# Seven products instead of eight for the second MLP matrix, with its sums on VectorE and by DMA, and a 16-byte pitch of the normed inputs

## The chip, the cores and the metric

One core of a Trainium2 chip runs the whole kernel. The metric is the device time of one execution in microseconds (us). The engines in the text: PE (TensorE, matrix products), DVE (VectorE), ACT (ScalarE), POOL (GpSimd, here only a queue that issues DMAs and a few fills) and SP (SyncE, the queue that issues most DMAs).

## What is computed

One decoder layer for 512 prompt tokens and 8 sample tokens, 520 columns in all, with 1024 features and 4096 inner features of the MLP. The part that the change touches:

```python
x = x + g1 * (merged @ w_out)
h2 = rmsnorm(x, norm2_g) * (1 + sc2) + sh2
ff = square(relu(h2 @ w_ff1)) @ w_ff2        # [1024, 4096], [4096, 1024]
x = x + g2 * ff
y = rmsnorm(x, final_norm_g)
```

Before it stand the input projection `w_in` (64 tiles of 128 output features), two recurrent branches, and their output matrices. Everything is float32.

## The kernel before

Activations lie as features x tokens: a tile is 128 features by 520 columns, `HALF` is 260. A float32 product is made of two-part operands: `whi`, `wlo` of the weights (`_split_w`: a cast on ACT, L68, and a subtraction on DVE, L69) and hi, lo of the activations (`split`, L146 and L147). `products` (L100) then issues three matmuls, hi hi, hi lo and lo hi, for each half of 260 columns, each with its own weight load. `gemm` runs over the inner tiles into one PSUM tile `mm` of two banks (one per half); `pmm` holds two such tiles.

A weight tile is 1024 rows x 128 columns (512 KB). `weights` gets the list of all tiles in the order of their use; `take_w` keeps loads three tiles ahead of the splits and splits two ahead (`AHEAD`). The loads go out on SP's queue into `wst` (four buffers); the split tiles lie in `whl` (two buffers).

The normed input `h` and the second norm's scaled input `h2` are [128, 8, T2] tiles, T2 = 530 floats: 520 columns, then nine columns of shifts and one to fill up. `h2` is scaled by the root mean square only after the product (L891).

`mlp` runs in two halves of the inner features. In a half, 16 tiles of `w_ff1` make 16 inner tiles: product, scale by `rs` (L891), the samples' shift (L892), relu with the prompt's shift (L893, L894), square on DVE (L895), split (L146, L147) into the pool `ab`. Then each of the eight output tiles takes two weight tiles of `w_ff2`, 96 matmuls, and `residual` (L808 and on) adds the gated sum to `x[m]`. In the second half the final norm follows each output tile (`final_tile`: transposes, squares, the product with `gbc`); the last output tile is done half by half of the tokens (`last_tile`), and the rows are scaled and written out.

The order on each engine follows the program's order by priority and readiness, fixed ahead of the run; `urgent` puts what frees a PSUM bank ahead of what was issued shortly before.

## Time and profile before

| | |
|---|---|
| runs | 1074.60, 1074.03, 1071.95 us; median 1074.03 |
| profiled execution | span 1070.9 us from the first to the last instruction |
| PE, PEld | 1035.1 us (97%), 998.7 us (93%) busy |
| DVE, ACT, POOL | 603.9 us (56%), 446.8 us (42%), 25.6 us (2%) busy |
| granted clock of PE | mean 0.996 |
| chain that ended last | PE 93%, of it the matmuls of L100 82% of the span |
| DMA | 136.34 MB, mean 127 GB/s |

A PE row's duration is the latency of one matmul; since matmuls are pipelined, what one costs is the distance between the starts of two. In rows of groups the number after `x` is the count, then busy time in us and the mean of one in ns, then idle time ahead of them and what ended it. In rows in order of time stand start, duration, engine, line, operation and operands (out<-in).

### The profile page before, as it was taken

How to read it: one execution, taken by the hardware profiler on the slowest of the kernel's cores; microseconds unless marked ns; L12 is line 12 of the kernel's file. 1: busy time of each engine (PE TensorE's matmuls, PEld its weight loads, DVE VectorE, ACT ScalarE, POOL GpSimd, SP SyncE). 2: the span in 40 equal slices, each digit the busy share in tenths (PEclk: the TensorE clock that was granted, in tenths of full speed). 3: DMA queues.
4: the chain of work that ended last, by engine and by line, in shares of the span. 5: the costliest groups of instructions: out<-in, count | busy, mean ns of one | idle time of the engine just before them, and what ended most of it. 6: DMA issues, size and time to landing. Idle time of an engine off the chain costs nothing.

```text
span 1070.9 us, 23934 instructions
## 1 busy us (share of the span) xinstructions
PE 1035.1 (97%) x10132; PEld 998.7 (93%) x10132; DVE 603.9 (56%) x1429; ACT 446.8 (42%) x897; POOL 25.6 (2%) x68
## 2 busy tenths in 40 slices
PE   3899999999999999989999999999999999999996
PEld 1799999999999999989999999999999999999996
DVE  6568678596786867464333346665542235554333
ACT  5445744663574364351222234444421124443332
POOL 2200000000000000110000000000000000000000
PEclk9999999999999999999999999999999999999999
DMA  9953444334333324695555573333323333332312
GB/s 278 252 170 101 121 123 125 111 121 141 107 120 113 110 92 142 186 281 165 160 158 160 158 210 86 92 90 89 94 84 99 85 94 93 86 96 82 96 44 80
DMA packets 239212, 136.34 MB, mean 127 GB/s; under 512 B 5214, under 2 KB 233750, under 8 KB 239098
## 3 DMA queue, kind: packets, MB, share of 16 engines
q1 hardware_dynamic: 237218, 129.75, 42.3%
q0 software_dynamic: 1888, 5.07, 1.5%
q8 instruction: 79, 1.29, 0.5%
q14 instruction: 27, 0.22, 0.1%
HBM read 123.61 MB, written 11.26 MB: 126 GB/s over the span
## 4 chain that ended last, share of the span: by engine, by line
PE 93%; SPq 3%; DMA 2%; ACT 1%; DVE 1%; issue 0%; ACTq 0%; DVEq 0%
PE mm L100 82%; PE ps L339 2%; SPq L1061 2%; PE pb L685 1%; DMA wst<-in_w_in_dram 1%; PE ps L544 1%; DMA wm<-in_w_mod_dram 1%; PE pt L628 1%; PE pt L617 1%; SPq L62 1%; PE ps L512 1%; PE pt L630 1%; PE ps L582 0%; PE pt L611 0%; DMA vd<-vs 0%
## 5 line engine op out<-in xcount | busy, mean ns | idle before, releaser
L100 PE MATMUL mm<-h,whi 128*128 128x260 f32 (+1 forms) x3072 | 518.2, 287 | 1.4 <-ACT X L120 1.4
L100 PEld LDWEIGHTS mm<-h,whi 128*128 128x128 f32 x3072 | 432.2, 190 | 7.2 <-issue 3.4
L100 PE MATMUL mm<-h,wlo 128*128 128x260 f32 (+1 forms) x1536 | 318.7, 287 | 0.0
L68 ACT CAST whi<-wst 128x1024 fp32r<-128x1024 f32 x152 | 159.3, 1048 | 333.8 <-PE mm L100 288.4
L69 DVE TENSOR_TENSOR wlo<-wst,whi 128x1024 fp32r<-128x1024 f32 x152 | 185.6, 1221 | 118.7 <-ACT whi L68 116.7
L100 PEld LDWEIGHTS mm<-h,wlo 128*128 128x128 f32 x1536 | 241.4, 190 | 1.7 <-issue 1.0
L100 PE MATMUL mm<-a,whi 128*128 128x260 f32 x1024 | 171.3, 286 | 0.0
L100 PEld LDWEIGHTS mm<-a,whi 128*128 128x128 f32 x1024 | 142.3, 189 | 1.6 <-issue 1.4
L100 PE MATMUL mm<-b,whi 128*128 128x260 f32 x768 | 125.0, 284 | 0.0
L100 PEld LDWEIGHTS mm<-b,whi 128*128 128x128 f32 x768 | 105.9, 189 | 1.6 <-issue 1.6
L100 PE MATMUL mm<-a,wlo 128*128 128x260 f32 x512 | 105.0, 283 | 0.0
L100 PEld LDWEIGHTS mm<-a,wlo 128*128 128x128 f32 x512 | 79.5, 188 | 0.2 <-issue 0.2
L100 PE MATMUL mm<-b,wlo 128*128 128x260 f32 x384 | 78.9, 284 | 0.0
L100 PEld LDWEIGHTS mm<-b,wlo 128*128 128x128 f32 x384 | 59.7, 188 | 0.0
L808 DVE SCALAR_TENSOR_TENSOR ma<-mm,modT,ma 128x260 f32<-128x260 f32 x23 | 11.2, 488 | 70.4 <-PE mm L100 66.0
L893 ACT ACTIVATE t<-t,fsh 128x512 f32<-128x512 f32 x32 | 23.0, 723 | 57.4 <-DVE t L891 57.4
L895 DVE TENSOR_TENSOR t<-t 128x520 f32<-128x520 f32 x32 | 22.3, 700 | 20.9 <-ACT t L894 20.9
L147 DVE TENSOR_TENSOR a<-t,a 128x520 fp32r<-128x520 f32 x32 | 21.9, 696 | 12.8 <-ACT a L146 12.8
L146 ACT CAST a<-t 128x520 fp32r<-128x520 f32 x32 | 19.6, 626 | 18.4 <-DVE t L895 10.0
L796 DVE TENSOR_TENSOR t<-mm,t 128x520 f32<-128x520 f32 x8 | 5.6, 699 | 37.0 <-PE ps L355 37.0
L147 DVE TENSOR_TENSOR b<-t,b 128x520 fp32r<-128x520 f32 x24 | 16.6, 699 | 14.1 <-ACT b L146 14.1
L359 DVE TENSOR_REDUCE mods<-ps 128x9 f32<-128x36 f32 x32 | 6.1, 190 | 32.6 <-PE ps L355 32.5
(301 smaller groups left out, 1008.5 us busy)
## 6 DMA issues: line engine op xcount, KB each, us to landing
wst<-in_w_in_dram SPq DMA_DIRECT2D x64, 512.0 KB
wst<-in_w_ff_dram SPq DMA_DIRECT2D x64, 512.0 KB
wst<-in_w_mod_dram SPq DMA_DIRECT2D x32, 512.0 KB
wm<-in_w_mod_dram SPq DMA_DIRECT2D x16, 512.0 KB
st<-in_state_hgrn_dram SPq DMA_DIRECT2D x8, 512.0 KB
vb<-vd SPq DMA_DIRECT2D x8, 512.0 KB
out_dram<-st SPq DMA_DIRECT2D x8, 512.0 KB
wst<-in_w_branch_a_dram SPq DMA_DIRECT2D x8, 512.0 KB
```

What stands on the lines that cost most here:

```text
L62: self.nc.sync.dma_start(st, src[r0:r0 + 1024, c0:c0 + 128].rearrange("(k p) n -> p k n", p=128))
L68: self.nc.scalar.copy(hi, st)
L69: self.nc.vector.tensor_tensor(lo, st, hi.bitcast(F32), OP.subtract)
L100: self.last_product = self.nc.tensor.matmul(ps[:, s, :c.stop - c.start], x, y[:, c], start=first and n == 0, stop=last and n == 2)
L146: self.nc.scalar.copy(hi, full)
L147: self.nc.vector.tensor_tensor(lo, full, hi.bitcast(F32), OP.subtract)
L339: nc.tensor.matmul(ps[r:r + 32, :n], self.cT[:, k, :], w[:, k, :], start=k < 4, stop=k >= KO - 4)
L512: nc.tensor.matmul(po[j:j + 32, c:c + 128], fkq[:, 2], st[:, b], start=True, stop=True)
L808: nc.vector.scalar_tensor_tensor(x[:, :HALF], ps[:, 0, :HALF], g[:, 0:1], x[:, :HALF], OP.mult, OP.add)
L893: nc.scalar.activation(t[:, :L], t[:, :L], AF.Relu, bias=sh[:, 0:1])
L895: nc.vector.tensor_tensor(t, t, t, OP.mult)
L1061: nc.sync.dma_start(raw[k][:, :, j * 128:(j + 1) * 128], w[r:r + 1024, c:c + 128].rearrange("(k p) n -> p k n", p=128))
```

## The change

Four things change; line numbers in names above are those of the kernel before.

*The second MLP matrix.* Inner features go in four quarters of eight inner tiles. A quarter's inner tiles are taken in four pairs (even, odd tile), the 520 columns as two halves, and the output tiles in four pairs `m`. For each pair of output tiles, seven sums of products take the place of eight. With B11, B12 for the even inner tile's two halves and B21, B22 for the odd one's, `hidden` makes seven forms of a pair of inner tiles, B11, B21, B22, B11 - B12, B12 - B22 - B11, B12 - B22 and B21 + B12 - B22 - B11, each in two parts; the square moves from DVE to ACT (into `f8`). `_split_pair` makes the weights' sums: group 0 is the plain first block, group 1 the plain second column block, group 2 two sums made by accumulating DMAs on POOL's queue (the second overwrites what the first reads, and so waits for it), group 3 two sums on DVE. `product` issues 12 matmuls (4 inner tiles x 3 parts) of 260 columns for product `j`. Products 1, 6, 5, 3 gather in one bank of `mm`, products 7 and 4 in the other, product 2 in the bank `pb`; between them `added` copies the partial sums out (`snap`, ACT, urgent) and adds them to `x`: on DVE, and for two of them a pair in the first three quarters by an accumulating DMA. The samples' columns gather in `zs`.

*The order.* `plan` writes out the order of tiles of the first matrix (`unit`, a quarter of a tile's product) and of products. After a quarter's last tile come the inner tiles 0 to 2 of products 1 of pair 0, 1 of pair 1, 2 and 7 of pair 0, then inner tile 3 of the same four. The next quarter's first tile is cut up between the last products.

*Pools.* Split weight tiles lie in turn in `whl` and in a new pool `sw` (two buffers each). `sw` also holds the raw pairs of `w_ff2` (pair 2's lie in `wst`), loaded as four transfers of 256 KB a pair. Small tiles of the recurrent part move from `sm` and `consts` to `hg` and `hc`, whose place is free again for the MLP.

*Pitch and end.* T2 is 532 floats. The final norm works on pairs of output tiles (`final_pair`), the last pair half by half of the tokens; `gbc` is loaded on SP's queue at the last quarter.

```diff
-NM = 9           # conditioning rows: the prompt and the samples
-T2 = T + NM + 1  # columns with the shifts beside the activations
+NM = 9
+T2 = T + NM + 3
...
+    def split_pool(self):
+        self.nsplit += 1
+        return self.sw if self.sw and self.nsplit % 2 else self.whl
...
+    FORM = {1: 0, 2: 1, 3: 2, 5: 3, 6: 4, 7: 5, 4: 6}
+    GROUP = {1: (0, 0), 2: (1, 0), 4: (1, 1), 7: (2, 0), 5: (2, 1), 6: (3, 1), 3: (3, 0)}
...
+    def plan(self):
+        late, end = (0, 1, 2), (3,)
+        first = [(0, 1), (1, 1), (0, 2), (0, 7)]
+        rest = [(0, 4), (0, 6), (1, 2), (1, 7), (0, 5), (1, 4), (0, 3), (1, 6), (2, 1), (1, 5), (2, 2), (1, 3), (2, 7),
+                (3, 1), (2, 4), (2, 6), (3, 2), (3, 7), (2, 5), (3, 4), (2, 3), (3, 6), 0, (3, 5), 1, (3, 3), 2, 3]
+        items, entries = [], []
+        for q in range(4):
+            items += [("u", q, j, c) for j in range(int(q > 0), KO) for c in range(4)]
+            items += [("p", q, *x, ks) for ks in (late, end) for x in first]
...
+    def _load_pair(self, key):
...
+            for n in range(2):
+                self.nc.sync.dma_start(t[:, 4 * n:4 * n + 4], v[e, :, n])
...
+    def _split_pair(self, key):
+        nc, g = self.nc, key[4]
+        a, b = self.raw[key[1:3]]
+        x11, x21, x12, x22 = a[:, :4], a[:, 4:], b[:, :4], b[:, 4:]
+        if g == 0:
+            hi, lo = (self.sw.tile([128, 4, 128], F32R, name=n, bufs=2) for n in ("xhi", "xlo"))
+            nc.scalar.copy(hi, x11)
+            nc.vector.tensor_tensor(lo, x11, hi.bitcast(F32), OP.subtract)
+            nc.gpsimd.dma_start(x11, x21, accum_op=OP.add)
+            nc.gpsimd.dma_start(x21, x22, accum_op=OP.add)
+            return hi, lo
+        if g == 3:
+            nc.vector.tensor_tensor(x22, x22, x11, OP.add)
+            nc.vector.tensor_tensor(x12, x12, x22, OP.add)
+            del self.raw[key[1:3]]
+        return self._split_w(a if g == 2 else b, self.split_pool())
...
+    def product(self, q, m, j, ks):
...
+        ps = (st["A"] if j == 2 else st["mm"][:, int(j in (7, 4))])[:, :HALF]
+        for k in ks:
+            w, (ah, al) = 4 * part + k if g else k, self.ff[k]
+            f = self.FORM[j]
+            for n, (x, y) in enumerate(((hi, ah), (hi, al), (lo, ah))):
+                self.nc.tensor.matmul(ps, x[:, w], y[:, f], start=j in (1, 7, 2) and k == 0 and n == 0,
+                                      stop=k == 3 and n == 2, skip_group_check=True)
...
+    def hidden(self, q, j, ps):
...
+        f = self.f8
+        nc.scalar.activation(f[:, 2 * e:2 * e + 2], self.two(t), AF.Square)
+        if e == 0:
+            self.forms(*self.ff[k], f[:, 0:1], 0, 1)
+            return
+        self.forms(*self.ff[k], f[:, 2:4], 1, 3)
+        for n, a, op, b in ((6, f[:, 1], OP.subtract, f[:, 3]), (5, f[:, 6], OP.subtract, f[:, 0]),
+                            (7, f[:, 2], OP.add, f[:, 5]), (4, f[:, 0], OP.subtract, f[:, 1])):
+            nc.vector.tensor_tensor(f[:, n], a, b, op)
+        self.forms(*self.ff[k], f[:, 4:8], 3, 7)
+
+    def added(self, q, m, j, ps, s):
...
+        def plus(t, c, part):
+            if q == 3:
+                nc.vector.tensor_tensor(x[t][:, c], x[t][:, c], part, OP.add)
+            else:
+                nc.gpsimd.dma_start(x[t][:, c], part, accum_op=OP.add)
+
+        if j == 1:
+            s[1] = self.snap(ps, "s1", g[0], 2)
+        if j == 7:
+            s[7] = self.snap(ps[:, :n], "s7", g[1], 2)
+            nc.vector.tensor_tensor(zs[1], zs[1], ps[:, n:], OP.add)
...
```

Of the kernel before, what the change touches and what calls it, by code (L numbers as in the profile page):

```python
# [6 lines left out]
F32 = mybir.dt.float32  # L7
# [38 lines left out]
class Kernel:  # L46
# [6 lines left out]
    # ---- weights: a tile is 1024 rows x 128 columns, in two parts that fp32r carries exactly  # L53
    def weights(self, specs):
        self.wspecs = specs
        self.wstage, self.wsplit = {}, {}
        self.wnext_load = self.wnext_split = self.wcur = 0

    def _load_w(self, key, pool):
        src, r0, c0 = key[:3]  # L60
        st = pool.tile([128, KO, 128], F32, name="wst")
        self.nc.sync.dma_start(st, src[r0:r0 + 1024, c0:c0 + 128].rearrange("(k p) n -> p k n", p=128))  # L62
        return st
# [11 lines left out]
    def take_w(self, key):  # L75
        n = self.wcur
        assert self.wspecs[n] == key, (n, self.wspecs[n], key)
        last = n
        for _ in range(AHEAD):  # tiles that go to the products as they are take no place in the split tiles' pool
            last += 1  # L80
            while last < len(self.wspecs) and self.wspecs[last][3:] == (WHOLE,):
                last += 1
        while self.wnext_split < min(last + 1, len(self.wspecs)):
# [4 lines left out]
            whole = self.wspecs[self.wnext_split][3:] == (WHOLE,)  # L88
            self.wsplit[self.wnext_split] = st if whole else self._split_w(st, self.whl)
# [4 lines left out]
    def products(self, ps, w, a, first, last, extra=0, halves=(0, 1)):  # L94
        """ps += W^T a, for one 128 x 128 tile of W and one tile of a, both in two parts."""
# [7 lines left out]
    def gemm(self, keys, acts, extra=0):  # L103
        """[128, 2, HALF (+ extra in the second)] of W^T act for one tile of 128 output features."""
# [10 lines left out]
    # ---- ScalarE's tables: what needs the exponential's and the root's stays together between sigmoids  # L115
# [15 lines left out]
    def urgent(self):  # L131
        """Ahead of what is emitted shortly before: what a product's place in PSUM waits for."""
# [17 lines left out]
    def rsqrt_small(self, x, n, p=128, w=16):  # L150
        """x[p, n] ** -0.5 to float32's accuracy (x normal and positive)."""
# [12 lines left out]
    # ---- constants and parameters  # L164
# [13 lines left out]
    def constants(self):  # L178
        nc, sb = self.nc, self.consts
        # masks of the pairs (s, t) inside 32 x 32 diagonal blocks, by the level that carries them  # L180
# [20 lines left out]
    def transpose_in(self, out, rows, n):  # L201
        """rows [n, 128] -> out [128, n]"""
# [8 lines left out]
    def bounds(self):  # L211
        """What depends on parameters through the exponential: HGRN2's lower bounds, RG-LRU's decay rates."""
# [4 lines left out]
        pl = self.consts.tile([128, 16], F32, name="pl")  # L217
# [3 lines left out]
        sb = self.consts  # L221
# [16 lines left out]
    def decays(self):  # L238
        """c8 = 8 softplus(-lam); log1p(e) = 2 atanh(e / (2 + e))"""
# [15 lines left out]
    def parameters_mod(self):  # L255
        """The norms' scales and the conditioning's bias (plus one where a scale comes of it)."""
# [29 lines left out]
    def parameters_in(self, ra, rb, rc):  # L286
        sb = self.consts
# [13 lines left out]
    # ---- conditioning  # L301
# [9 lines left out]
    def cond(self):  # L311
        """silu of the conditioning rows, transposed, with room for 32 of them."""
# [5 lines left out]
        self.cT = self.consts.tile([128, KO, 32], F32, name="cT")  # L318
# [50 lines left out]
    # ---- the input, its norm, and its transpose  # L369
# [8 lines left out]
    def norm_x(self):  # L378
# [3 lines left out]
        junk = lambda: self.pmm.tile([128, 2, 512], F32, name="mm").rearrange("p a b -> p (a b)")  # noqa: E731  # L382
# [20 lines left out]
    def transposed(self, k):  # L403
        """Columns k * 128 .. + 128 of the rows, transposed where they are."""
# [15 lines left out]
    def affine_split(self, k, prompt, sample):  # L420
        """The normed input's tile k times 1 + scale, plus the shift, in two parts."""
# [7 lines left out]
        v = lambda t: t[:, :L].rearrange("p (t f) -> p t f", f=128)  # noqa: E731  # L429
# [4 lines left out]
    # ---- HGRN2  # L434
# [9 lines left out]
    def head_f(self, h, ps):  # L444
        """f = max(lb, floor) + (1 - lb) sigmoid(fa), k = (1 - lb) sigmoid(-fa)"""
# [43 lines left out]
    def head_sample_v(self, h, v):  # L489
# [3 lines left out]
        vs = self.sm.tile([NB, 128], F32, name="vs")  # L493
# [8 lines left out]
    def head_sample(self, h, st, vb, fkq):  # L502
# [5 lines left out]
        # four samples' states at a time, each with all samples' queries in its own 32 columns of the array  # L508
# [4 lines left out]
        ev = self.sm.tile([128, 256], F32, name="sev")  # L513
# [7 lines left out]
    def head_prompt(self, h, f, X, q, v, og):  # L521
        nc = self.nc
        # values as [s, v]
# [6 lines left out]
        # levels: Q_b[t] = q_t * f's from the b-block's start to t, K_b[s] = k_s * f's after s to the block's end,  # L530
# [634 lines left out]
```

More of the change, by code (lines that the diff above doesn't have):

```diff
@@ L867, in norm2 @@
         nc = self.nc
[L868 to L869 removed]
+        self.rs = self.misc.tile([128, T], F32, name="rs", bufs=1)
+        parts = self.misc.tile([128, 4, T], F32R, tag="f8", name="sqs", bufs=1)
+        parts = parts[:, 0], parts[:, 1]
+        nc.scalar.copy(parts[0], self.sq)
+        nc.vector.tensor_tensor(parts[1], self.sq, parts[0].bitcast(F32), OP.subtract)
         for s in range(2):
@@ new lines, in mlp @@
+    def mlp(self):
+        nc, tc = self.nc, self.tc
+        self.close_pool()
+        self.early.close()
+        self.ffp = self.ctx.enter_context(tc.tile_pool(name="ffp", bufs=1, reuse_waits="tile"))
+        self.zs = self.consts.tile([128, KO, NB], F32, name="zs")
+        nc.vector.memset(self.zs, 0.0)
+        self.ng = self.consts.tile([128, KO], F32, name="ng")
+        nc.vector.tensor_scalar(self.ng, self.modT[:, 40:48, 0], -1.0, None, OP.mult)
+        self.ff, self.pairs, self.taken = {}, {}, {}
+        for what, q, a, b, *ks in self.items:
+            if what == "u":
+                self.unit(q, a, b)
+                continue
+            if (q, a, b, ks[0][0]) == (3, 0, 1, 0):
+                self.final_open()
+            self.product(q, a, b, *ks)
```

323 lines of the change are left out of this document (203 added, 120 removed).

## The prediction

> **What bounds the kernel now.** I read the page first (who is busy, what the chain that ended last consists of), then the busy time by stage, then single rows.
>
> ```profile
> span 1070.9 us, 23934 instructions
> PE 1035.1 (97%) x10132; PEld 998.7 (93%) x10132; DVE 603.9 (56%) x1429; ACT 446.8 (42%) x897; POOL 25.6 (2%) x68
> PE 93%; SPq 3%; DMA 2%; ACT 1%; DVE 1%; issue 0%; ACTq 0%; DVEq 0%
> 690.00:795.00 105.00, 105.00 (x855) 105.00 (x854) 60.40 (x88) 46.18 (x88) 0.00 (x0) 1.00 0.32 91
> 795.00:875.00 80.00, 80.00 (x668) 80.00 (x667) 23.68 (x42) 14.31 (x14) 0.00 (x0) 1.00 0.33 93
> 875.00:970.00 95.00, 95.00 (x771) 95.00 (x771) 54.06 (x80) 41.01 (x80) 0.00 (x0) 1.00 0.32 90
> 970.00:1055.00 85.00, 85.00 (x713) 84.87 (x713) 30.20 (x57) 27.51 (x84) 0.00 (x0) 1.00 0.22 63
> ```
>
> TensorE carries 93% of the chain. The four windows are the MLP: first matrix, second matrix, and both again for the other half of the inner features. Columns are the stretch, then PE, weight load, VectorE, ScalarE and GpSimd busy time, granted clock, DMA share and GB/s. PE is never idle there, the clock is 1.00, VectorE is 30 to 58% busy, GpSimd 0. So each matmul less is worth its issue interval, and each new PE wait costs in full.
>
> **The matmuls removed.** Counts by form, and two beats of the second matrix:
>
> ```profile
> L100 PE MATMUL mm<-a,whi 128*128 128x260 f32 x512 | 86.4, 286 | 0.0
> L100 PE MATMUL mm<-b,whi 128*128 128x260 f32 x512 | 83.0, 282 | 0.0
> L100 PE MATMUL mm<-b,wlo 128*128 128x260 f32 x256 | 53.0, 284 | 0.0
> L100 PE MATMUL mm<-a,wlo 128*128 128x260 f32 x256 | 52.8, 283 | 0.0
> 858.19 0.49 DVE L808 SCALAR_TENSOR_TENSOR ma<-mm,modT,ma 128x260 f32<-128x260 f32 x1 [3.69 <-PE mm L100]
> 869.71 0.49 DVE L808 SCALAR_TENSOR_TENSOR ma<-mm,modT,ma 128x260 f32<-128x260 f32 x1 [3.69 <-PE mm L100]
> ```
>
> These are the 1536 matmuls of the second matrix (512 + 512 + 256 + 256); 286 ns is a latency, not a price. The residual comes every 11.52 us for 96 matmuls, so one costs 120.0 ns. Afterwards there are 4 quarters x 4 pairs x 7 products x 4 inner tiles x 3 parts = 1344, of the same shape (260 columns, own weight load). 192 x 0.120 = **-23.0 us**.
>
> **The pitch.** A normed-input tile starts every 2120 bytes, so every second one is 8 bytes off a multiple of 16; afterwards (2128) none is. Two whole products (a gate on the normed input, then a branch on aligned tiles), and the gate's inner tiles 2 to 5, whose beats start at these times:
>
> ```profile
> 524.66 6.04 PE mm L100 x48
> 531.38 5.96 PE mm L100 x48
> ...
> 526.15 0.65 PE L100 MATMUL mm<-h,whi 128*128 128x260 f32 x4
> 526.87 0.65 PE L100 MATMUL mm<-h,whi 128*128 128x260 f32 x4
> 527.61 0.64 PE L100 MATMUL mm<-h,whi 128*128 128x260 f32 x4
> 528.32 0.66 PE L100 MATMUL mm<-h,whi 128*128 128x260 f32 x4
> 529.07 0.64 PE L100 MATMUL mm<-h,whi 128*128 128x260 f32 x4
> ```
>
> Six matmuls take 0.72 us on tile 2, 0.74 on 3, 0.71 on 4, 0.75 on 5: odd tiles pay up to 5 ns a matmul by these rounded starts; the whole products differ by 0.08 us over 24 odd matmuls, 3.3 ns. 96 products read the normed inputs (64 of w_in, 32 of the first MLP matrix), 2304 odd matmuls. At 2 ns this is **-4.5 us**; ends 0 (the offset isn't the cause) and -7.6 (3.3 ns). I take the low side because a head's chain has other work beside the products.
>
> **What it adds on PE's path.** Durations for these steps:
>
> ```profile
> 876.47 1.23 DVE L69 TENSOR_TENSOR wlo<-wst,whi 128x1024 fp32r<-128x1024 f32 x1 [4.61 <-ACT whi L68]
> 877.62 0.69 DVE L891 TENSOR_TENSOR t<-mm,rs 128x520 f32<-128x520 f32 x1
> 879.20 0.70 DVE L895 TENSOR_TENSOR t<-t 128x520 f32<-128x520 f32 x1 [0.69 <-ACT t L894]
> 880.59 0.70 DVE L147 TENSOR_TENSOR a<-t,a 128x520 fp32r<-128x520 f32 x1 [0.69 <-ACT a L146]
> ...
> 878.34 0.72 ACT L893 ACTIVATE t<-t,fsh 128x512 f32<-128x512 f32 x1 [1.83 <-DVE t L891]
> 879.93 0.63 ACT L146 CAST a<-t 128x520 fp32r<-128x520 f32 x1 [0.77 <-DVE t L895]
> 881.33 1.05 ACT L68 CAST whi<-wst 128x1024 fp32r<-128x1024 f32 x1 [0.78 <-PE mm L100]
> ...
> L875 ACT ACTIVATE rs<-ps,epsc 128x260 f32<-128x260 f32 x2 | 0.8, 472 | 0.0
> L811 DVE TENSOR_TENSOR rst<-mm,modT 128x8 f32<-128x8 f32 x15 | 2.3, 154 | 0.0
> 1061.61 0.41 PE L918 MATMUL ps<-ident,ma 128*128 128x128 f32 x2 [0.67 <-DVE ma L945]
> ```
>
> (1) End of a quarter's first-matrix tiles. Before, 15 other inner tiles came ahead of the last one (90 matmuls, 10.8 us), over a chain of 3.7 us (877.62 to 881.29). Now the last tile must also pass the seven forms, and 36 matmuls on the three older inner tiles plus 9 cover it: 45 x 0.12 = 5.4 us until product 7's last step needs the form B12 - B22 - B11. The chain: scale 0.72, relu with its sample columns 0.75, square 0.63, then four sums on VectorE of half a 520 row each, some 0.36 us apart (1.4), cast of four forms 1.07, their low part 1.2: 5.8 us, plus 0.3 from the last matmul's start to VectorE's. If VectorE does the low part of the first two forms ahead of the sums, as written, 1.2 us more. The stall is 0.6 (sums first) to 2.1 us (as written); an unlucky weight split of 1.2 ahead of it makes 3. I take 1.3, nearer the middle since the order on the engine is by priority: 4 x 1.3 = **+5.2** (2.4 to 12).
>
> (2) Product 4 of pair 0 follows product 7 of pair 0 and adds to the same PSUM bank, which ScalarE must first copy (0.47) and VectorE read (0.15); with the matmul's latency and PE's restart after VectorE (0.15 in the last row: VectorE ended at 1061.46) 1.0 us a quarter: **+4.0** (3 to 6). Other pairs have another pair's product (1.44 us) between.
>
> (3) Splits have four buffers in turn, two ahead. The next quarter's first tile takes the buffer of pair 2's last sums, read until one product before: cast 1.05 + low part 1.2, while PE has 1.44 plus the 0.5 until it needs the low part: 0.7 x 3 = **+2.1** (1 to 5). Three other splits a quarter have 2.9 us for the same 2.3; a VectorE instruction in the way breaks that: 12 x 0.1 = **+1.2** (0 to 7).
>
> (4) The last pair of the last quarter runs products 6, 5, 3 on one bank with nothing between: 0.7 + 0.9 = **+1.6**.
>
> (5) VectorE. A pair costs it four low parts (0.7 + 3 x 1.2), two weight sums of 0.7 and 2.3 us of residual: 8.0, four pairs 32 us of the 45 that PE has in quarters 1 to 3: covered. In the last quarter two residual sums of 0.4 (no DMA), the sample rows (0.6) and the final norm's products (2 x 0.7 + 0.3) come on top: 44 us busy, some 40 in sequence (rows of one engine overlap by 0.08: 876.47 + 1.23 against 877.62), against PE's 39.5 plus the waits above. The cover is nearly gone; I put **+2** (0 to 8). ScalarE stays under 30 us.
>
> (6) The tail behind the last matmul:
>
> ```profile
> 1060.98 0.48 DVE L945 SCALAR_TENSOR_TENSOR ma<-mm,modT,ma 128x252 f32<-128x252 f32 x1
> 1062.05 0.28 ACT L923 ACTIVATE junk<-ps 128x128 f32<-128x128 f32 x1
> 1064.39 0.18 DVE L955 RECIPROCAL fr<-fr 128x3 f32<-128x3 f32 x1 [0.36 <-ACT fr L954]
> 1064.60 1.04 ACT L959 ACTIVATE fx<-fx,fr 128x896 f32<-128x896 f32 x1 [0.25 <-DVE fr L955]
> ```
>
> Two tiles are squared instead of one (2 more at 0.4, and a sample row 0.4), the last row's scale is 1024 wide instead of 896 (+0.15), a separate 128-wide product goes (-0.3): **+0.7** (0 to 2).
>
> (7) The DMA sums: 32 on weights, 24 on residuals, all on GpSimd's queue, where the second sum of a pair waits for the first and holds up what is queued behind (residual sums, the next pair's). Nearest rows, from a stage at twice the traffic:
>
> ```profile
> t<-obT_d POOLq DMA_DIRECT2D x8, 260.0 KB, 7.0
> gbc<-in_final_norm_g_dram POOLq DMA_DIRECT2D x1, 512.0 KB, 5.0
> ```
>
> The tightest are pair 2's: its first split can run when pair 0's first weights are free, 17 us before the split that needs both sums is due (18 us ahead of its product). Two at 5 to 7 us take 10 to 14: **0**. The Trainium skill ("DMA: Bandwidth & Descriptors", section "Anatomy of one DMA") fits 2.0 us plus bytes over 436 GB/s, 2.6 us for 256 KB; the sum would stay the same by it. No run here shows an accumulating transfer yet.
>
> Loads of the second matrix come as 64 transfers of 256 KB instead of 32 of 512 on SP's queue, with DMA 33% busy: 0. The tiles that move to other pools keep their two buffers: 0. In the first-matrix stretches VectorE has 7.2 us of new and old work per 11.8 us: 0.
>
> **Sum**: -23.0 - 4.5 + 5.2 + 4.0 + 2.1 + 1.2 + 1.6 + 2 + 0.7 = -10.7. The runs' median (1074.0) lies 3.1 us above the profiled span of 1070.9; the span becomes 1060.2 and the median 1063.3, say **1064**.
>
> **Rivals.**
> A. The waits are mostly covered (sums ahead of low parts, no VectorE collision): (1) 2.4, (2) 3, (3) 1, (4) 1.4, (5) and (6) 0: 7.8 of 27.5 given back, 1054. For it: VectorE is idle 42% even in the first-matrix stretches. Against: its queue is in order and a split holds it 1.2 us.
> B. VectorE becomes the bound of the product stretches: (1) at 3 each, (3) at 5 + 7, (5) at 8: 12 + 4 + 12 + 1.6 + 8 + 0.7 = 38 lost, +11, 1085 at the far end; half the excess gives no change, 1074. For it: 40 of 39.5 us in the last quarter. Against: the other three have 27% to spare.
> C. Slower, by GpSimd's queue alone: a DMA sum that takes over 8.5 us makes pair 2's second sum late (2 x 8.5 = 17); at 11 us each product 7 of pair 2 waits 5 us and pair 3's, queued behind, as long again: 10 x 4 = 40 us, 1103; it eats the gain of 10.7 from about 10 us a sum on (2.7 us a quarter). For it: 7.0 us rows on that queue. Against: those moved DRAM data at 160 to 210 GB/s; here it is 90. The Trainium skill ("TensorE: Matmul & The Clock Gate", Part 1) has the clock fall to half after an idle window of some 3.4 us; C's waits would then cost more than counted, those of (1) to (4) not. No wait of this length is in this trace's MLP.
> D. The pitch does nothing: 1068.
>
> **Chances.** Forecast 0.48 (1058 to 1069), A 0.22, D 0.08, B 0.14 (half of it within 0.3%), C 0.08. A change of 0.3% (3.2 us) is about what a measurement of this kernel can tell from none. Faster 0.74 (forecast, A, D less their upper ends), same 0.14, slower 0.12. 80% range 1053 (A) to 1076 (half of B); the forecast's own is 1058 to 1069.
>
> **What would show it.** Right: 1344 matmuls on 260-column forms at 120 ns; beats of odd input tiles equal to even ones; PE idle of about a microsecond before product 7's last step and product 4 of pair 0, and at the next quarter's first tile; POOL-queue sums landing within 7 us; VectorE over 85% busy in the last quarter. Wrong: PE waits of 3 us and more behind VectorE's low parts (B) or behind weights that a DMA sum completes (C), or no gaps at all (A).

## The result, and the profile after

| | before | after |
|---|---|---|
| median of the runs, us | 1074.32 (1071.95 to 1074.8) | 1104.16 (1099.81 to 1105.42) |
| ratio, 95% interval | | 1.0281 (1.0256 to 1.0306) |
| span of the profiled execution, us | 1070.9 | 1098.0 |
| mean granted TensorE clock there | 0.996 | 0.981 |

The change makes the kernel 2.8% slower: 30 us by the medians, 27.2 by the profiled executions. The forecast was 10 us faster. From the page of the changed kernel, the busy shares and the rows of PE and of the granted clock in 40 slices:

```profile
PE 1028.7 (94%) x9940; PEld 983.2 (90%) x9940; DVE 694.9 (63%) x1624; ACT 531.4 (48%) x1041; POOL 73.6 (7%) x123
PE   3999999999999999999999999989997899789895
PEclk9999999999999999999999999999998999999898
```

192 instructions fewer on PE, and yet 27 us more span: PE, 97% busy before, is at 94%, and the dents in its row stand in the last third, where the granted clock has its dents too. Busy time by stretch (columns as in the prediction: PE, weight load, VectorE, ScalarE, GpSimd, granted clock, DMA share, GB/s). The first row is the first matrix of quarter 1; the others are the second matrix of quarters 1, 2 and 4:

```profile
676.50:726.50 50.00, 50.00 (x411) 50.00 (x410) 35.95 (x60) 30.71 (x56) 0.00 (x0) 1.00 0.26 75
726.50:777.00 50.50, 41.99 (x307) 40.20 (x306) 30.39 (x55) 22.66 (x35) 12.41 (x15) 0.93 0.60 128
828.00:879.00 51.00, 42.36 (x306) 40.56 (x305) 29.80 (x55) 22.30 (x34) 12.90 (x15) 0.90 0.59 127
1033.00:1085.40 52.40, 45.50 (x344) 43.03 (x343) 35.19 (x84) 30.59 (x99) 3.43 (x4) 0.93 0.12 21
```

The first matrix runs as before: PE full, clock 1.00. In the second PE stands still for 8.5 us of 50 (6.9 of 52 in the last quarter), at a mean clock of 0.90 to 0.93, and no other engine is full: VectorE is busy 60%, in the last quarter 67%. The waits of TensorE's instructions by what released them (us in total, times, longest):

```profile
PE mm L995 <- DVE zs L1071: 12.5, 9, 2.2
PE pb L995 <- ACT ff3h L1007: 8.6, 4, 2.2
PE mm L995 <- DVE ma L1063: 4.1, 7, 0.6
PE mm L995 <- DVE zs L1059: 3.3, 5, 0.8
PE pb L995 <- DVE ma L1063: 2.3, 4, 0.6
PE pb L995 <- DVE ff3l L1008: 1.8, 4, 0.5
PE mm L110 <- DVE wlo L73: 1.0, 3, 0.4
```

The first row is, but for two waits of the last pair, the wait of product 6 for the sum of product 4 (`added`, L1063): the releaser is inferred, and L1071, another pair's product 5, is only the next instruction behind that sum on VectorE. The shorter waits of the same kind stand in the third row, under L1063 itself.

For a ledger I added up the distances between successive matmul starts in the MLP. What a distance has above 0.124 us is a wait if it is more than 0.145 us, and a slow step if it is 0.06 to 0.145 us; the rest is plain distance. A slow step is at half clock if the trace's granted clock is 0.5 there (a matmul then takes 0.22 us); the others are single steps at full clock. From before to after:

| part | us |
|---|---|
| all up to the first matrix (its first 270-column matmul at 682.00, then 676.41) | -5.6 |
| plain distances of the second matrix (1536 matmuls, then 1344) | -20.9 |
| plain distances of the first matrix | -1.8 |
| waits of TensorE (none, then 42) | +42.2 |
| slow steps at half clock (0, then 9.5) | +9.5 |
| slow steps at full clock (1.8, then 3.4) | +1.7 |
| transposes, small distances | -0.4 |
| behind the last matmul (10.2, then 12.6) | +2.4 |
| sum | 27.1 |

So the removed matmuls did save time, and so did the part ahead of the MLP; two things outweighed them. The first row is not the pitch alone. Between the matmuls 4750 and 5000, where TensorE waits for a tile of `w_in`, the changed kernel takes 26.4 us against 30.0 before, and between 6500 and 6750, ahead of the MLP, 28.8 against 27.1. All eleven traces of the changed scheme show it (26.2 to 29.1, and 27.8 to 29.1); with the pitch alone (e1_pitch, e1_again, below) the first is 30.5 and 31.2, the second 27.1. The wait in the chain of before, after and e1_pitch:

```profile
446.68 11.56 DMA wst<-in_w_in_dram
443.81 9.06 DMA wst<-in_w_in_dram
444.32 12.16 DMA wst<-in_w_in_dram
```

Now the waits in the MLP. TensorE's rows around the first quarter's end (start, duration, operands, idle time before and its releaser):

```profile
728.74 0.28 PE L995 MATMUL mm<-ff3h,xlo 128*128 128x260 f32 x1
731.16 0.38 PE L995 MATMUL pb<-ff3h,whi 128*128 128x260 f32 x1 [2.15 <-ACT ff3h L1007]
732.04 0.39 PE L995 MATMUL pb<-ff3l,whi 128*128 128x260 f32 x1 [0.50 <-DVE ff3l L1008]
733.12 0.58 PE L995 MATMUL pb<-ff0h,whi 128*128 128x260 f32 x1 [0.58 <-DVE ma L1063]
733.50 0.42 PE L995 MATMUL pb<-ff0l,whi 128*128 128x260 f32 x1
733.72 0.42 PE L995 MATMUL pb<-ff0h,wlo 128*128 128x260 f32 x1
...
737.45 0.39 PE L995 MATMUL mm<-ff0h,whi 128*128 128x260 f32 x1 [0.76 <-DVE zs L1059]
739.74 0.39 PE L995 MATMUL mm<-ff0h,whi 128*128 128x260 f32 x1 [0.58 <-DVE ma L1063]
```

Product 2 of pair 0 waits 2.31 + 0.76 us for the forms of the last inner tile. What stands ahead of them on VectorE and ScalarE:

```profile
725.09 1.22 DVE L73 TENSOR_TENSOR wlo<-wst,whi 128x1024 fp32r<-128x1024 f32 x1 [0.99 <-ACT whi L72]
726.23 0.69 DVE L1022 TENSOR_TENSOR ft<-mm,rs 128x520 f32<-128x520 f32 x1
...
728.94 0.62 ACT L953 CAST xhi<-wst 128x512 fp32r<-128x512 f32 x1 [0.27 <-PE mm L995]
729.46 0.47 ACT L1003 ACTIVATE s<-mm,modT 128x260 f32<-128x260 f32 x1
729.83 0.62 ACT L1030 ACTIVATE f<-ft 128x520 f32<-128x520 f32 x1
730.49 0.62 ACT L1007 CAST ff3h<-f 128x520 fp32r<-128x520 f32 x1
```

The tile's chain begins at L1022, behind a weight's low part (L73); its square (L1030) comes behind a weight's cast (L953) and a copy of a partial sum (L1003). Further on, product 2 of pair 1 waits 0.74 for the sum of pair 0's, whose bank it takes; product 4 waits 1.01 behind product 7 (737.45); and product 6 (739.74) waits for VectorE to have read *product 4*, though product 4 lies in the other bank. Later in the quarter the same wait of product 6 is 1.47 and 2.22 us, because the sum of product 4 (L1063) stands behind a weight's low part on VectorE:

```profile
768.75 1.23 DVE L73 TENSOR_TENSOR wlo<-wst,whi 128x1024 fp32r<-128x1024 f32 x1 [0.26 <-ACT whi L72]
769.89 0.48 DVE L1063 SCALAR_TENSOR_TENSOR ma<-mm,modT,ma 128x260 f32<-128x260 f32 x1
```

Then the clock. From 733.50 on, the matmuls above start every 0.22 us instead of every 0.12. Three stretches of 3.41 us with that onset between the first two:

```profile
729.69:733.10 3.41, 0.88 (x3) 0.48 (x3) 2.88 (x6) 2.13 (x4) 1.47 (x3) 1.00 0.75 128
733.10:736.52 3.42, 3.40 (x15) 3.32 (x15) 1.63 (x2) 0.32 (x1) 2.36 (x3) 0.50 0.83 141
736.52:739.93 3.41, 2.07 (x15) 1.69 (x14) 0.75 (x3) 1.33 (x2) 0.86 (x1) 1.00 0.77 117
```

After a stretch in which TensorE issued three matmuls, the next runs at 0.50. The clock falls seven times in the MLP, behind the quarter's end or behind product 6 of pair 3, and twice it stays low for two stretches.

### The profile page after: what moved, and what is told of

It reads as the page before. It is cut to its first block, busy times and chain, and to the rows that moved or that the text cites. A ratio compares the mean times of both kernels' runs of the same rounds, so it can differ in the third digit from the quotient of the medians.

```text
span 1098.0 us, 24188 instructions
## 1 busy us (share of the span) xinstructions
PE 1028.7 (94%) x9940; PEld 983.2 (90%) x9940; DVE 694.9 (63%) x1624; ACT 531.4 (48%) x1041; POOL 73.6 (7%) x123
## 4 chain that ended last, share of the span: by engine, by line
PE 86%; DMA 3%; ACT 3%; DVE 3%; SPq 2%; issue 1%; DVEq 0%; ACTq 0%
PE mm L110 62%; PE mm L995 12%; PE pb L995 3%; PE ps L349 2%; DMA wst<-in_w_ff_dram 1%; PE pb L695 1%; PE ps L554 1%; ACT whi L72 1%; DVE wlo L73 1%; DMA wst<-in_w_in_dram 1%; DVE ma L1063 1%; DMA wm<-in_w_mod_dram 1%; PE pt L638 1%; PE pt L627 1%; SPq L66 1%
## 5 line engine op out<-in xcount | busy, mean ns | idle before, releaser
L73 DVE TENSOR_TENSOR wlo<-wst,whi 128x1024 fp32r<-128x1024 f32 x168 | 205.0, 1222 | 87.2 <-ACT whi L72 84.8
L110 PE MATMUL mm<-a,whi 128*128 128x260 f32 x512 | 85.0, 285 | 0.0
L110 PEld LDWEIGHTS mm<-a,whi 128*128 128x128 f32 x512 | 70.6, 188 | 1.4 <-issue 1.4
L110 PE MATMUL mm<-a,wlo 128*128 128x260 f32 x256 | 52.0, 284 | 0.0
L1037 DVE TENSOR_TENSOR f<-f 128x260 f32<-128x260 f32 x64 | 27.4, 428 | 27.6 <-ACT f L1030 27.0
L995 PE MATMUL mm<-ff0h,whi 128*128 128x260 f32 x80 | 25.9, 323 | 19.9 <-DVE zs L1071 12.5
L1024 ACT ACTIVATE ft<-ft,fsh 128x512 f32<-128x512 f32 x32 | 23.1, 724 | 42.9 <-DVE ft L1022 42.9
L110 PE MATMUL mm<-b,whi 128*128 128x260 f32 x256 | 41.9, 286 | 0.0
L110 PEld LDWEIGHTS mm<-a,wlo 128*128 128x128 f32 x256 | 39.4, 188 | 0.2 <-issue 0.2
L110 PEld LDWEIGHTS mm<-b,whi 128*128 128x128 f32 x256 | 34.9, 188 | 1.6 <-issue 1.6
L1003 ACT ACTIVATE s<-mm,ng 128x260 f32<-128x260 f32 (+1 forms) x32 | 15.1, 471 | 30.7 <-PE mm L995 30.7
L1003 ACT ACTIVATE s<-mm,modT 128x260 f32<-128x260 f32 (+1 forms) x32 | 15.1, 472 | 26.1 <-PE mm L995 26.0
```

The costliest lines, as they stand in the source:

```text
L73: self.nc.vector.tensor_tensor(lo, st, hi.bitcast(F32), OP.subtract)
L110: self.last_product = self.nc.tensor.matmul(ps[:, s, :c.stop - c.start], x, y[:, c], start=first and n == 0, stop=last and n == 2)
L995: self.nc.tensor.matmul(ps, x[:, w], y[:, f], start=j in (1, 7, 2) and k == 0 and n == 0, stop=k == 3 and n == 2, skip_group_check=True)
L1003: self.nc.scalar.activation(t, ps, AF.Copy, scale=scale)
L1024: nc.scalar.activation(t[:, :L], t[:, :L], AF.Relu, bias=sh[:, 0:1])
L1037: nc.vector.tensor_tensor(f[:, n], a, b, op)
```

## The experiments

The ledger for all of them (us; waits and slow steps in the profiled execution, the median and the ratio to the kernel before with its interval). The ratio is to runs of the kernel before that were taken beside each:

| kernel | median | ratio | waits | slow steps | of them at half clock |
|---|---|---|---|---|---|
| before | 1074.32 | | 0 | 1.8 | 0 |
| after | 1104.16 | 1.0281 (1.0256 to 1.0306) | 42.2 | 13.0 | 9.5 |
| e1_pitch | 1068.58 | 0.9952 (0.9938 to 0.9966) | 0 | 1.7 | 0 |
| e1_again | 1070.14 | 0.9968 (0.9958 to 0.9978) | 0 | 1.7 | 0 |
| e2_warm_b | 1090.58 | 1.0163 (1.0133 to 1.0194) | 26.0 + 13.0 filled | 6.0 | 2.1 |
| e3_hold | 1100.40 | 1.0258 (1.0234 to 1.0281) | 41.2 | 13.6 | 10.0 |
| e4_banks | 1078.72 | 1.0049 (1.0032 to 1.0066) | 26.3 | 8.7 | 5.4 |
| e5_chain | 1093.87 | 1.0175 (1.0149 to 1.0201) | 40.6 | 11.8 | 8.4 |
| e6_nosum | 1088.71 | 1.0131 (1.0103 to 1.0158) | 33.3 | 8.7 | 5.0 |
| e8_combo | 1079.73 | 1.0048 (1.0034 to 1.0061) | 26.3 | 8.4 | 5.9 |
| e9_free | 1070.59 | 0.9967 (0.9954 to 0.9980) | 20.0 | 6.5 | 3.4 |
| e10_pool | 1077.55 | 1.0041 (1.0026 to 1.0055) | 24.2 | 7.1 | 2.7 |
| e11_last | 1069.35 | 0.9963 (0.9949 to 0.9976) | 18.8 | 4.9 | 1.5 |
| e12_order | 1072.48 | 0.9987 (0.9976 to 0.9999) | 21.6 | 8.3 | 4.2 |

**The pitch alone.** In the kernel before, `T2 = T + NM + 3`.

> The kernel before with one edit: the operand tile's pitch of 532 instead of 530 columns, so that odd inner tiles begin on a multiple of 16 bytes. Theory (the pitch is real and is worth what the matmuls of odd inner tiles show, 122.3 against 120.35 ns): the first 270-column matmul starts 5 to 6 us earlier, the first MLP product loses another 1 us or less, and the whole is 5.5 to 7 us faster, 1067 to 1069 us. Rival (the earlier start of the MLP in the changed kernel came from its moved pools and weight tiles, not from the pitch): within 1.5 us of before, and odd and even inner tiles stay 2 ns apart.

> The kernel before with the pitch alone once more, on the same chip as e11_last: 1068 to 1069 us. It tells whether the scheme without its waits (e11_last) is worth anything beyond the pitch: 2 us or more faster if the theory's 1065 to 1067 holds, equal or slower otherwise.

Measured -5.2 and -3.4 us (0.9952 and 0.9968 of 1074): real, under what I expected, about the -4.5 of the prediction. The mean distance of matmuls on the normed input ahead of the MLP falls from 121.4 to 120.2 ns, in these two traces as in the changed kernel; over 3072 matmuls that is 3.6 us, and the first MLP matrix gives another 1.3. But the first 270-column matmul starts only 2.5 and 0.8 us earlier (679.50 and 681.21), not 5 to 6, because waits ahead of it came out longer, that for `w_in` among them. The rival of e1_pitch is right for a part: some 3.6 us of the changed kernel's early start, less 1.8 lost just ahead of the MLP, are not the pitch. The moved pools and the other loads are the likely cause; no run separates them. A gate's 48 matmuls on the normed input, 6.04 us before against 5.96 for a branch, take in e1_pitch, by the chain in order of time:

```profile
516.12 5.96 PE mm L100 x48
...
522.76 5.97 PE mm L100 x48
```

Gate and branch are equal now.

**Work in place of the idle time.** In the changed kernel (shortened; further lines hold the products beside it to the order that they had):

```diff
+        if (m, j, ks[0]) in ((0, 2, 3), (3, 6, 0))[:1 + (q < 3)]:
+            warm = self.ppt.tile([128, 512], F32, name="pt")
+            for _ in range(16):
+                w1 = self.nc.tensor.matmul(warm[:, :HALF], self.ones_r, self.ff[2][0][:, 0], start=True, stop=True)
+                self.behind(w1, self.last_product)
```

> The changed kernel with 16 matmuls of 260 columns, whose result nobody reads, put into two waits of each quarter: between product 1 of pair 1 and the last inner tile of product 2 of pair 0 (wait of 2.31 + 0.76 us), and ahead of product 6 of pair 3 (2.22 us; not in the last quarter). The order of all other matmuls is that of the changed kernel. It takes away the idle time and not the lateness. Theory (the half clock is the price of those two waits): no stretch at half clock between the quarters' ends, mean granted clock back to 0.995, 10 to 14 us faster than the changed kernel, 1090 to 1094 us. Rival (the clock falls for another reason, such as the load of the product stage itself): clock stays at 0.98 and the time at 1104 us, or up to 7 x 1.9 = 13 us more where the added matmuls hold up work that was ready.

1090.6, 13.6 us less than the changed kernel (9.3 by the profiled executions), within the theory's range. The slow steps at half clock go from 9.5 us to 2.1; of the seven falls of the clock two are left, behind the first matrix of quarters 2 and 4. Three of the four runs had a granted clock of 0.994 to 0.995 and took 1088.8 to 1090.6 us; the fourth, at 0.982, took 1098.0. The same place as above:

```profile
729.62 2.08 PE L996 MATMUL pt<-ff2h,ones_r 128*128 128x260 f32 x16
731.93 0.38 PE L1003 MATMUL pb<-ff3h,whi 128*128 128x260 f32 x1 [0.23 <-ACT ff3h L1018]
...
733.90 0.39 PE L1003 MATMUL pb<-ff0h,whi 128*128 128x260 f32 x1 [0.58 <-DVE ma L1074]
734.13 0.28 PE L1003 MATMUL pb<-ff0l,whi 128*128 128x260 f32 x1
734.25 0.29 PE L1003 MATMUL pb<-ff0h,wlo 128*128 128x260 f32 x1
```

The forms are as late as before, but what follows starts every 0.12 us. TensorE has more work here than in the changed kernel and the clock falls less often, so the rival, the load itself, is out: the half clock is a price of the idle time, on top of it.

**The two banks.** In the changed kernel:

```diff
+            if j == 7 and q < 3:
+                st["B"] = self.pps.tile([128, 512], F32, name="ps")
-        ps = (st["A"] if j == 2 else st["mm"][:, int(j in (7, 4))])[:, :HALF]
+        ps = (st["A"] if j == 2 else st["B"] if j in (7, 4) and q < 3 else st["mm"][:, int(j in (7, 4))])[:, :HALF]
```

> The changed kernel with the accumulator of products 7 and 4 in a PSUM tile of its own in the first three quarters (two tiles that stand unused there), instead of the second bank of the pair's tile. Theory (product 6 waits for the sum of product 4 only because both banks are one tile): the waits ahead of product 6 of all pairs vanish, 0.74 + 0.74 + 1.47 + 2.22 = 5.2 us a quarter and 15.5 us in three, with them the second fall of the clock in each (3 x 3.4 us at half speed, 5 us), and product 6 of pair 0 can run in the wait at the quarter's end (about 1 us of it each time): 1078 to 1090 us. Rival (VectorE is the bound: its sums stand behind the weights' low parts whatever the bank): the waits move to products 3 and 5 or to the next pair and the time stays within 5 us of 1104. Rival (the sums by DMA make it slow): no change either, since none of them is touched.

1078.7, 25 us less (19.7 by the profiled executions), and waits down by 15.9 against an expected 15.5. Some of TensorE's waits there:

```profile
PE pb L997 <- ACT ff3h L1009: 5.4, 4, 2.2
PE mm L997 <- DVE zs L1073: 2.3, 3, 0.9
PE mm L997 <- DVE wlo L73: 2.3, 3, 0.8
```

The 12.5 us for L1071 are 2.3 (L1073 here, all in the last quarter, which was left alone). The largest single part of the waits is a dependency between two halves of one tile that touch different banks. The match with 15.5 is partly luck: product 6's 15.8 us in three quarters are gone, the wait for the forms is 1.07 shorter each time, since product 6 of pair 0 now runs in it, but TensorE now waits 0.77 and 0.91 us a quarter, 5.0 in three, for weights' low parts; net of these the tie is worth some 11 us of waits. To that extent the rival (VectorE is late with something else instead) is right; for the rest it falls, since VectorE had the same sums to do.

**The order of the queues.** Two attempts to bring the last hidden tile's chain forward with scheduling dependencies only (excerpts; the remarks in them are mine).

```diff
 e3_hold
+            held(nc.scalar.copy(hi, x11), 1)                 # raw pairs 2 and 3: behind the square
+            held(nc.vector.tensor_tensor(x22, x22, x11, OP.add), 0)   # behind the samples' addition
+            if tag == "s1" and self.hold:
+                self.behind(ins, self.hold[1])               # snapshot of product 1: behind the square
 e5_chain
+        self.held(self.nc.vector.tensor_tensor(lo, st, hi.bitcast(F32), OP.subtract), 0)   # any low part
+        c, v = self.forms(*self.ff[k], f[:, 2:4], 1, 3)      # the rest: behind these casts
```

> The changed kernel with the last hidden tile's chain put first at the quarter's end: on ScalarE the two snapshots of product 1 and the later pairs' weight casts behind the square, on VectorE the sum of raw weights behind the samples' addition. Theory (the wait of 3.07 us at the quarter's end is the queue on VectorE and ScalarE ahead of the chain, not the chain's own length): the wait falls to about 1 us in each of the four quarters, -6 to -9 us, and the half clock behind it goes (20 of the 27 us at half speed), -8 more: 1087 to 1096 us. Rival (VectorE as such is the bound: what is held back is late afterwards): the wait moves to the products that need the held weights, and the time is within 3 us of 1104.

> The changed kernel with the queue ahead of the quarter's last hidden tile ordered anew, after a first attempt (e3_hold) that left the weight's low part in front of it and put other work right behind the square: low parts of weights behind the samples' addition, snapshots of product 1, the sums of raw weights and the casts of pairs 2 and 3 behind the casts of the last forms. Nothing is removed. Theory (the chain is late because 1.2 us of a weight's low part, then snapshots and casts, stand ahead of it on VectorE and ScalarE): the chain starts 1.2 to 1.8 us sooner and runs 1 us shorter, the waits of 2.31 + 0.76 + 0.74 us at each quarter's end fall under 1.5 us together, 4 x 2.5 = 10 us, and the half clock that follows them in each quarter goes, another 6 to 8: 1086 to 1092 us. Rival (VectorE is full there, so that what is put behind is late instead): the time stays within 3 us of e3_hold's 1100.

e3_hold gave 3.8 us, within the spread: a weight's low part still stood ahead of the chain's first instruction, and the casts came right behind the square, ahead of the forms. In e5_chain the waits for the forms fell from 10.4 us to 1.4, and 10.3 us were gained by the medians, just outside the expected range. The profiled execution gains only 3.2, with 40.6 us of waits; the other runs have a higher clock: its four runs took 1096.6, 1095.1, 1092.6 and 1088.6 us at clocks 0.983, 0.988, 0.988 and 0.995. The idle time came back one step further on (2.3 and 3.3 us in the changed kernel):

```profile
PE pb L1002 <- DVE ma L1075: 7.8, 4, 2.0
PE mm L1002 <- DVE zs L1071: 6.6, 5, 2.0
```

VectorE's rows at that place:

```profile
728.60 1.29 DVE L966 TENSOR_TENSOR wst<-wst 128x512 f32<-128x512 f32 x2
729.80 0.42 DVE L1049 TENSOR_TENSOR f<-f 128x260 f32<-128x260 f32 x1
730.14 0.69 DVE L958 TENSOR_TENSOR xlo<-wst,xhi 128x512 fp32r<-128x512 f32 x1
730.74 0.48 DVE L1075 SCALAR_TENSOR_TENSOR ma<-pb,modT,ma 128x260 f32<-128x260 f32 x1
```

Product 2 of pair 0 was done at 729, its sum waits on VectorE until 730.74 behind the work that had been put back, and the next user of that bank waits for it. The theory is right on where the forms' wait came from and wrong on what its removal is worth; the rival, VectorE full at that place, is right there.

**Without the weights' sums.** The two accumulating transfers and the two additions of `_split_pair` taken out.

> The changed kernel without the sums of raw weights: the 32 accumulating transfers and the 32 additions on VectorE (0.69 us each, 22 us) are left out, so products use unsummed weights and the output is another. Theory (sums of weights are off the path, but for the two that stand ahead of the last hidden tile's chain): 0 to 8 us faster than the changed kernel, 1096 to 1104 us, product 6 still waits for product 4. Rival (VectorE's added work is what the waits are made of): 20 us or more, 1084 us or less. Rival (the transfers' way over the GpSimd queue is the cost): the same size, with the waits of products 5, 6, 7 gone.

15.5 us less, between the two. The row of product 6's waits falls from 12.5 to 10.0, that of the forms from 8.6 to 6.1, the slow steps at half clock from 9.5 to 5.0: work on VectorE that stands ahead of something urgent lengthens waits whose cause lies elsewhere. I had the share of VectorE's queue too low, and the rest stays when it is gone. The transfers went together with the additions, so this run does not separate the two. Against the transfers: no wait of TensorE in the changed kernel ends with one, and they land in 3.4 us (weights) and 3.8 to 5.1 (residuals):

```profile
wst<-wst POOLq DMA_DIRECT2D x32, 256.0 KB, 3.4
ma<-s POOLq DMA_DIRECT2D x12, 130.0 KB, 3.8
ma<-s POOLq DMA_DIRECT2D x12, 126.0 KB, 5.1
```

**Putting it together.** e9_free is e4_banks (and pairs 0 and 1 of the last quarter) with product 2 of odd pairs in the unused bank `pt`; e8_combo has e5_chain's order as well; e10_pool is e9_free with `nc.gpsimd.tensor_tensor` for the two additions; e11_last gives pair 1 of the last quarter `pt` too; e12_order has another list of products:

```diff
-                st["A"] = self.ppb.tile([128, 512], F32, name="pb")
+                st["A"] = self.ppt.tile([128, 512], F32, name="pt") if q < 3 and m % 2 else self.ppb.tile([128, 512], F32, name="pb")
 e11_last
-                ... if q < 3 and m % 2 else ...
+                ... if m == 1 or q < 3 and m == 3 else ...
 e12_order
-        rest = [(0, 4), (0, 6), (1, 2), (1, 7), (0, 5), ...
+        rest = [(1, 2), (0, 6), (1, 7), (0, 4), (0, 5), ...
```

> The changed kernel with e4_banks (in the last quarter too, for pairs 0 and 1), e5_chain, and product 2 of odd pairs in the bank that stands unused there, instead of the one bank that it shares with even pairs (first three quarters). All arithmetic is that of the changed kernel. Theory: from e4_banks's 1078.7, the waits at the quarters' ends 3 x 1.5 + 2.5, the wait for the shared bank 3 x 0.74, products 6 of the last quarter 1.5, and the 20 us at half clock that were left, about 8: 1058 to 1064 us, faster than before and than the pitch alone (1068.6). Rival (a floor that lies in VectorE's or ScalarE's share): 1070 us or more.

> e8_combo without the new order of VectorE's and ScalarE's queues: own tiles for the accumulators of products 7 and 4 (first three quarters, and pairs 0 and 1 of the last), product 2 of odd pairs in its own bank. In e8_combo 2.6 us of each quarter went to product 6 of pair 0, whose weight part had been put behind the forms; e5_chain showed the same work coming back as a wait of 2.1 us for the sum of product 2. Theory (give TensorE other ready products there rather than hurry the chain, and hold no weight back): the waits of 1.23 + 0.76 and 0.74 us per quarter of e4_banks go in three quarters, 8 us, products 6 of the last quarter 1.5, and the half clock behind them, 5 to 8: 1061 to 1068 us, faster than before. Rival (VectorE is full at the quarters' ends, so any order only moves the wait): 1076 us or more, as e4_banks and e8_combo.

> e9_free with the two sums of raw weights per pair, which VectorE does (0.69 us each, 32 of them), on GpSimd. Theory (e6_nosum, without sums at all, was 15 us faster than the changed kernel, so VectorE's queue makes a part of the waits): 0 to 6 us faster than e9_free. Rival (GpSimd's sums take much longer than 0.69 us and make the weight parts of products 5, 6, 3 and 7 late, or slow VectorE's own work): 5 us or more slower than e9_free, with waits of TensorE for those weights' casts.

> e9_free with product 2 of pair 1 in its own bank in the last quarter too, so that the last quarter's beginning can run in the order of the other three. Theory: of e9_free's waits in the last quarter (1.23 + 0.76 + 0.74 + 0.26 us) about 1.5 us go, and the 6.8 us at half clock behind them, 3 us: 1065 to 1067 us, some 7 us faster than before. Rival (the wait moves to the last bits of the forms, and the clock falls all the same): 1069 to 1071 us.

> e11_last with the list of products begun by product 2 of pair 1, then 6 of pair 0, 7 of pair 1, 4 and 5 of pair 0, instead of 4, 6 of pair 0, 2, 7 of pair 1, 5 of pair 0: the weight part of product 2 of pair 1 is split before that of product 6 of pair 0. Theory (any ready product serves at the quarter's end): within 2 us of e11_last. Rival (an earlier split puts one more low part ahead of the last hidden tile's chain on VectorE): 3 us or more slower, with the wait ahead of the last inner tile of product 1 or 2 longer than 1.5 us.

e8_combo missed by 16 us and is no better than e4_banks. The waits for the forms' high parts are down to 2.0 us, but product 6 of pair 0, now free to fill the gap, waits for the weight that had been put back (7.0 us in three quarters):

```profile
PE mm L1004 <- ACT whi L72: 7.0, 3, 2.4
```

Without that order e9_free gains 9 us on it, to 1070.6; it fell 2.6 us short of the range. e10_pool is 7 us slower, the rival's size: GpSimd takes 1.36 and 1.71 us for an addition that VectorE does in 0.69, and VectorE's low part of a raw block goes from 686 to 826 ns (e9_free's row, then e10_pool's rows):

```profile
L954 DVE TENSOR_TENSOR xlo<-wst,xhi 128x512 fp32r<-128x512 f32 x14 | 9.6, 686 | 1.1 <-ACT xhi L953 0.8
```

```profile
L954 DVE TENSOR_TENSOR xlo<-wst,xhi 128x512 fp32r<-128x512 f32 x14 | 11.6, 826 | 5.3 <-ACT xhi L953 5.3
L960 POOL TENSOR_TENSOR wst<-wst 128x512 f32<-128x512 f32 x16 | 27.3, 1706 | 1.3
L959 POOL TENSOR_TENSOR wst<-wst 128x512 f32<-128x512 f32 x16 | 21.7, 1358 | 233.1 <-DVE wlo L73 226.9 <-DVE zs L1082 6.2
```

The Trainium skill ("SBUF — State Buffer", section "SBUF: two separate sides") says that a VectorE instruction with two SBUF inputs and a GpSimd one that reads SBUF lock each other out; these rows agree, though no run here separates the lock from other causes.

e11_last, at 1069.4, lies in its rival's range, not in the theory's, and within the spread of e9_free: the clock falls once instead of twice, but the waits for the low parts of the last forms grow from 3.4 to 4.3 us, as the rival said. e12_order is 3 us slower than it, the rival's size, but not through the wait that the rival named: the waits at the quarter's end are 1.1 us at most, and a new one of 1.2 to 1.9 us stands in pair 3.

e9_free and e11_last beat the kernel before by 3.5 to 4 us and the changed one by 34. Against the pitch alone, on the same chip, e11_last is 0.8 us faster (1069.35 and 1070.14, ranges overlapping): no difference that these runs show. Its MLP, from the first 270-column matmul to the end, is not faster: 389.3 us against 387.5 in e1_again. It starts 3.0 us earlier (678.20 against 681.21), with the shorter wait for `w_in` of all kernels of the changed scheme. By these two traces the plain distances of the second matrix are 21.5 us shorter; 18.8 us of waits, 3.1 more in slow steps and 2.4 at the end use that up.

## Why the prediction was wrong

- *The matmuls removed, -23.0*: right in number and price, 1344 matmuls at 120.1 ns in the mean. The plain distances fall by 20.9 only, for 22 of the 1536, but 8 of the 1344, start 0.02 us behind a transpose, and waits and slow steps are counted from 0.124 us.
- *The pitch, -4.5*: right, -3.4 to -5.2 alone. That the moved pools and the loads are worth 0 ahead of the MLP was not: 3.6 us less in one stretch there, 1.8 more in another.
- *(1), quarter's end, +5.2 (2.4 to 12)*: the mechanism was right, the size was not: 3.07 us a quarter, 12.3. I gave one weight split in the way its price (3 us a quarter) and then took the middle; the trace has that split at 725.09, and copies and casts ahead on ScalarE besides. It was also product 2 that waited, not product 7, since the program put it first.
- *(2), product 4 behind product 7, +4.0*: right, 1.01 to 1.06 a quarter, 4.2.
- *(3)*: 0.52 x 3 = 1.5 for the 2.1 of the next quarter's first tile. The mechanism is right and the size partly luck: the terms written there, 1.05 + 1.2 - 1.44 - 0.5, give 0.3 and not 0.7. The three other splits a quarter cost nothing visible for 1.2.
- *(4), the last pair, +1.6*: 0.85 + 1.04 = 1.9, right.
- *(5), VectorE in the last quarter, +2*: the last quarter's stretch is 67% busy on VectorE, not over 85%; beyond (4), no wait there that the other quarters lack. What VectorE costs it costs in all quarters, by what stands ahead of an urgent sum, not by its load.
- *(6), the tail, +0.7 (0 to 2)*: 2.4; the terms written there add up to 1.05. The final norm's product of the half before (0.69 us) still ran on VectorE when the last residual was due, and the sample row's squares follow the four others in series.
- *(7), the sums by DMA, 0*: no wait of TensorE ends with one, and they land in 3.4 to 5.1 us, under the 8.5 of rival C, which falls.
- *Left out*: that product 6 waits for product 4's sum in the other bank of its tile, 0.74 + 0.74 + 1.47 + 2.22 = 5.2 us in the first quarter, 17.8 in all with 2.0 in the last. This is the step that failed: the list of what comes onto PE's path put it at nothing, without a reason. I took the two banks for independent, since each product's accumulation is, and never asked at which grain the program's waits are kept. Also left out: product 2 of pair 1 in pair 0's bank, 0.74 to 0.88 a quarter, 3.1.
- *Left out*: the clock, +9.5. I set it aside in one clause under rival C ("those of (1) to (4) not"), because each single wait was short. e2_warm_b shows that the idle time, in waits of 2.3 us and less, brings it about, and takes 7.4 of the 9.5 away.

Rival B came nearest (38 lost, 1085 at the far end, where 1104 was measured), but for a VectorE that is full, which no stretch shows; e6_nosum shows that its queue makes the waits longer. The sum of waits that I had, 16.8 with (6), was 44.6.

## What to carry to other kernels

When work is taken off an engine that is never idle, list for each new accumulator not only which instruction must read it but which other instructions the program's dependency tracking will tie to it: tiles, not banks, were the grain here, and a separate tile was worth 25 us. Price the idle time that is left as a sum over a few microseconds, not wait by wait: the clock fell here after waits of which none was longer than 2.7 us. Give the engine other ready work there before reordering the queues that make it late: e9_free did the first and gained 8 us on e4_banks; e5_chain and e8_combo did the second and moved the wait. And compare with the part of the change that is free of the new scheme, here the pitch: without it, e9_free and e11_last would look like a gain of seven products, which they are not.

## What the runs showed of the hardware

The half clock comes in steps of 3.413 us on a fixed grid within a trace, and it does not need an idle step. I count as idle what lies more than 0.12 us behind the last matmul's start. Over the eleven traces of the changed scheme, all 37 falls in the MLP follow a step at full clock in which TensorE was idle for 2.03 us or more (up to 3.22), and no such step that was not followed by a fall had more than 2.02. The Trainium skill ("TensorE: Matmul & The Clock Gate", Part 1) has the free-running window and the half rate after one idle window; the grid and the rate agree with these traces, but here a window idle for some six tenths was enough. So it should matter where on the grid a wait falls. That may be why runs of one kernel differ, e5_chain by 8 us between clocks of 0.983 and 0.995; with one trace for each kernel, this is not shown.
